# A decoder layer on one core: the scale columns' queue, 18 products of ones at the start, and four groups of small products moved by one or two steps

## The chip, the cores and the metric

The kernel runs on one core of a Trainium2 chip. Its time is the device time of one execution in microseconds (us); of several executions the median is given. Five engines work side by side, each with its own list of instructions: TensorE (PE, matmuls; PEld is its loading of weights), VectorE (DVE), ScalarE (ACT), GpSimd (POOL) and SyncE (SP, which here issues most of the transfers). An instruction starts when those ahead of it on its engine are through and the semaphores that it waits for have come.

## The reference, cut to what matters

One step of a hybrid decoder layer over 576 tokens: 512 of a new sequence and 8 x 8 of running ones, model width 2048.

```python
x += W_out @ [gated_delta_heads(8) | mlstm_heads(4)](rmsnorm(x) @ W_in)
x += conv_ffn(rmsnorm(x))         # W_up, causal conv, gate, W_down; d_ff = 5632
y  = rmsnorm(x)
# gated delta, chunks of 128 here: with k normalised and decays from the gates,
#   lower = strict(beta * k k^T * decay);  X = (I + lower)^-1
#   v_new = X (v - w S);  o = qe S + (q k^T * decay) v_new;  S = S * gl + kd^T v_new
# mlstm: the like, with a normaliser and a running maximum
# both again for the 64 sample tokens, each from its own stored state
```

The outputs are y and the new states of heads and convolutions. All is in 32-bit floats.

## The kernel before, in words

Every large product W x is taken apart into high and low halves of W and x (in a 32-bit format that TensorE reads at full rate), and three products hi·hi, hi·lo and lo·hi are added up. ScalarE casts a weight block `raw` to its high part `wh` (L120), VectorE subtracts to get the low part `wl` (L121); a block holds 8 k-tiles of 128 rows. The 576 tokens lie in two halves of 288 columns, so a **step**, one k-tile in `dense_part`, is six products (`three`, L200), and a dense tile of 128 output rows is 16 steps.

TensorE's order is the order in which the code issues (`manual_schedule`); the other engines' order is set by a scheduler from priorities and dependences. Between the dense products stand the small ones of the gates and heads, written as generators: after each step `tick()` lets each running generator go on until its next `yield n`, which makes it pause n ticks. So `yield n` sets by how many steps of dense work a small product stands behind what its operands come from. Small products write to four rotating PSUM tiles (`psr`).

`startup` (L360) loads the scale columns `g1` (2048 floats, 8 KB, on GpSimd's queue), sets `ones`, and then, for 16 activation tiles, loads x on SyncE's queue, scales it to `ah` on ScalarE (L384) and takes the rest `al` on VectorE (L385). The weight blocks are loaded after x tiles 1, 7 and 15. The gates' weights are scaled on GpSimd (L396).

`gate_rows` computes the gates of all heads: 64 products (L446) after 20 ticks, the squares' sum (L455), then a chain of small operations on rows, then two products with `there` (L520), whose operand comes from L511. Later it issues the gates' rows, on which the heads begin.

`dn_head` is one gated-delta head. It transposes k (L683; sample part L689 to L691), which ScalarE reads eight times (L686 and L687), builds `U` from k·k (L710), then KQ from k·q (L721), then transposes v (L732; sample part L737), pauses `YI` = 8 ticks while `inverse` works (L866 and L873 are its masks and sums), and then goes through the four chunks (L751, L758, L762 to L765). `dn_sample` (L832 to L846) does the sample tokens: L832, its ScalarE reader L833, the casts `vp` and `kp` (L797, in `pack`), masks `vm` on GpSimd (L806), and a product per pair of sequences (L846) that updates the state (L849). `ml_head` and `ml_sample` do the mLSTM heads; L1092 is the product for the samples' normaliser, L1040 a division of an output, L1044 a transposition of it.

Of the kernel before, what the change touches and what calls it, by code (L numbers as in the profile page):

```python
# [15 lines left out]
P = 128  # L16
D = 2048
KT = 16
# [20 lines left out]
OPA = 1600  # L39
YI = 8  # L40
YJ = 20


G1, G2, G3, CW, DG, MG, FW, FBI, GB, AL, M0, NPAR = 0, 16, 32, 48, 144, 145, 153, 417, 505, 506, 507, 515
# [22 lines left out]
class Layer:  # L67
# [292 lines left out]
    def startup(self):  # L360
        nc, I = self.nc, self.I
        self.par = self.cp.tile([P, NPAR], F32, tag="par", name="par")
        g1 = self.cp.tile([P, KT], F32, tag="g1", name="g1")
        nc.gpsimd.dma_start(out=g1, in_=I["par"][:, G1:G1 + KT])
        self.ones = self.cp.tile([P, P], F32, tag="ones", name="ones")
        nc.vector.memset(self.ones, 1.0)
        nc.scalar.activation(self.rstd_tile()[:, 0:1], self.ones[:, 0:1], AF.Copy)
        self.eps6 = self.cp.tile([P, 1], F32, tag="eps6", name="eps6")
        nc.vector.memset(self.eps6, EPS)
        self.epsh = self.cp.tile([P, 1], F32, tag="epsh", name="epsh")  # L370
        nc.vector.memset(self.epsh, EPS * EPS * P)

        self.xh, self.xl, self.xs = [], [], []
        self.gw = self.r(shape=[P, KT, 32])
        acts = [self.new_act(k) for k in reversed(range(KT))][::-1]
        for k in range(KT):
            x = self.r()
            self.xs.append(x)
            nc.sync.dma_start(out=x, in_=I["xT"][k])
            if k in (1, 7, 15):  # L380
                self.load_unit()
            hi, lo = acts[k]
            g = g1[:, k:k + 1]
            nc.scalar.activation(hi, x, AF.Copy, scale=g)  # L384
            nc.vector.scalar_tensor_tensor(out=lo, in0=x, scalar=g, in1=hi.bitcast(F32), op0=ALU.mult, op1=ALU.subtract)  # L385
            self.xh.append(hi)
            self.xl.append(lo)
        for k in range(0, KT, 4):
            self.gate_weights(k, g1)
        nc.sync.dma_start(out=self.par, in_=I["par"])  # L390
# [38 lines left out]
    def gate_rows(self):  # L429
        nc, I, O = self.nc, self.I, self.O  # L430
# [79 lines left out]
        for s, t in quarters:  # L510
            V.scalar_tensor_tensor(out=t5[s, t], in0=y[s], scalar=cq[s, 4:5], in1=val[s], op0=ALU.mult, op1=ALU.add)  # L511
        edge.__exit__(None, None, None)
        yield 12
        R1, R2, R3 = self.r(), self.r(), self.r()
        for t in (R1, R2, R3):
            Pl.memset(t, 0.0)
# [143 lines left out]
    def dn_head(self, h, q, k, v, sz):  # L660
        nc, I, O = self.nc, self.I, self.O
# [52 lines left out]
        res = []  # L714
        inv = self.inverse(U, res, 0)
        next(inv)
        yield 1
        pr = self.psr()
        for c in range(NCH):
            sl, n = self.blk(c)  # L720
# [12 lines left out]
        for c in range(NCH):  # L733
            sl, n = self.blk(c)
            A.activation(vs[:, sl], pv[:, sl], AF.Copy, scale=irk[:, c:c + 1])
        pv = self.psr()
        nc.tensor.transpose(pv[0:64, 0:P], v[:, sl4], self.ident)  # L737
        A.activation(vss, pv[0:64, 0:P], AF.Copy, scale=irk[0:64, 4:5])

        yield YI  # L740
        yield from inv
        X, Xs = res
        sample = self.spawn(self.dn_sample(h, st, k, qe, KQ, Xs, cjc(4), kds, vss, gl))
# [109 lines left out]
    def inverse(self, U, res, more):  # L853
# [44 lines left out]
        def masked(i):  # L898
            m = U if i == len(LV) - 1 else self.r()
            Pl.tensor_tensor(out=c4(m), in0=c4(U), in1=self.bc4(self.con[:, C_LV + P * i:C_LV + P * i + P]), op=ALU.mult)  # L900
            return m

        m = masked(0)
        yield YJ + more
        self.tc.cur_priority -= PR
# [166 lines left out]
    def ml_sample(self, h, caug, kws, sT, gl, finish):  # L1072
        nc, O = self.nc, self.O
        V, A, Pl, mm = nc.vector, nc.scalar, nc.gpsimd, nc.tensor.matmul
        sl = slice(SEQ, NT)
        yield 2
        qc = self.r(shape=[P, 2, 257])
        for g in range(2):
            pr = self.psr()
            for j in range(4):  # L1080
                mm(pr[32 * j:32 * j + 32, 0:257], self.qim[:, 4 * g + j], caug[g][:, j], start=True, stop=True)
            A.copy(qc[:, g], pr[:, 0:257])
        yield 2
        pn = self.psr()
        mm(pn[0:64, 0:257], sT[0:64, sl], self.vas, start=True, stop=False)
        for g in range(2):
            mm(pn[32 * g:32 * g + 32, 0:257], self.pick[:, 0], qc[:, g], start=False, stop=True)
        fin = self.spawn(finish(pn, 4))
        bmk = self.con[0:64, C_BM:C_BM + NB]
        yield 4  # L1090
        pm = self.psr()
        mm(pm[:, 0:NB], kws, bmk, start=True, stop=True)  # L1092
        for b in range(NB):
            n1 = caug[b // 4][:, b % 4, 256:257]
            V.scalar_tensor_tensor(out=n1, in0=n1, scalar=gl[:, 4 + b:5 + b], in1=pm[:, b:b + 1], op0=ALU.mult, op1=ALU.add)
        kp = self.pack(kws, P, "kp", ("hhl", "hhl"))
        vp = self.pack(self.vas, 256, "vp", ("hlh", "lhh"))
        for g in range(4):
            vm = self.masked_rows(vp, g // 2, g % 2 * 2, 2)
            yield W  # L1100
            pr = self.psr()
            mm(pr, kp[:, g // 2], vm, start=True, stop=True)
            for i in range(2):
                b = 2 * g + i
                cc = caug[b // 4][:, b % 4, 0:256]
                V.scalar_tensor_tensor(out=cc, in0=cc, scalar=gl[:, 4 + b:5 + b], in1=pr[:, 256 * i:256 * i + 256], op0=ALU.mult, op1=ALU.add)
        for g in range(2):
            self.later(6, O["sC"][h, g], caug[g])
        while not fin[3]:
            yield 1  # L1110
# [628 lines left out]
```

## Time and profile before

| | |
|---|---|
| median of 3 runs | 2661.66 us (2661.35 to 2661.88) |
| the profiled execution | 2660.97 us, span 2659.2 us |
| TensorE busy, whole span | 2628.2 us (99%) |
| TensorE busy, 139 to 860 us (heads) | 714.58 of 721 us |
| TensorE busy, 860 to 2110 us | 1249.01 of 1250 us |
| TensorE's first product | at 8.50 us |
| granted TensorE clock, mean | 0.998 |

The profile is one execution. The waits of an engine are listed as "line waited for, total, times, longest". A row of the timeline gives start, duration, engine, line, operation and tiles; in square brackets stands how long the engine was idle before, and what ended it. "xN" is a run of N equal instructions; a product of plain 32-bit floats shows as two rows of TensorE. The busy time of matmuls overlaps, so their pace is read from their starts.

### The profile page before, as it was taken

How to read it: one execution, taken by the hardware profiler on the slowest of the kernel's cores; microseconds unless marked ns; L12 is line 12 of the kernel's file. 1: busy time of each engine (PE TensorE's matmuls, PEld its weight loads, DVE VectorE, ACT ScalarE, POOL GpSimd, SP SyncE). 2: the span in 40 equal slices, each digit the busy share in tenths (PEclk: the TensorE clock that was granted, in tenths of full speed). 3: DMA queues.
4: the chain of work that ended last, by engine and by line, in shares of the span. 5: the costliest groups of instructions: out<-in, count | busy, mean ns of one | idle time of the engine just before them, and what ended most of it. 6: DMA issues, size and time to landing. Idle time of an engine off the chain costs nothing.

```text
span 2659.2 us, 49165 instructions
## 1 busy us (share of the span) xinstructions
PE 2628.2 (99%) x20061; PEld 2584.9 (97%) x20061; DVE 2057.7 (77%) x3448; ACT 1083.3 (41%) x1697; POOL 461.6 (17%) x670
## 2 busy tenths in 40 slices
PE   8999999999999999999999999999999999999998
PEld 8999999999999999999999999999999999999997
DVE  6676666667765455599999999999999998988656
ACT  5333433434434333244444444444444443434224
POOL 2222322322322001111212222222222200000001
PEclk9999999999999999999999999999999999999999
DMA  5242322422323434343333333333333463342332
GB/s 206 83 126 87 130 84 78 131 86 85 98 85 106 154 121 135 129 137 114 109 109 109 109 108 108 106 108 107 108 108 109 133 231 90 119 137 71 123 98 100
DMA packets 112682, 304.05 MB, mean 114 GB/s; under 512 B 21928, under 2 KB 28216, under 8 KB 112456
## 3 DMA queue, kind: packets, MB, share of 16 engines
q1 hardware_dynamic: 108616, 292.20, 34.2%
q0 software_dynamic: 1600, 6.35, 0.7%
q8 instruction: 157, 2.57, 0.4%
q10 hardware_dynamic: 2240, 2.36, 0.2%
q14 instruction: 69, 0.57, 0.1%
HBM read 262.44 MB, written 38.42 MB: 113 GB/s over the span
## 4 chain that ended last, share of the span: by engine, by line
PE 96%; DVE 2%; ACT 1%; issue 0%; POOL 0%; DMA 0%; DVEq 0%; POOLq 0%
PE pd L200 38%; PE pr L1358 33%; PE pd L1358 13%; PE pr L200 4%; PE pr L1588 1%; DVE r L1623 0%; PE pr L918 0%; PE pr L258 0%; DVE wl L121 0%; PE pr L721 0%; PE pr L758 0%; ACT r L686 0%; PE pr L930 0%; PE pr L1055 0%; ACT r L687 0%
## 5 line engine op out<-in xcount | busy, mean ns | idle before, releaser
L120 ACT CAST wh<-raw 128x1024 fp32r<-128x1024 f32 (+1 forms) x392 | 403.2, 1029 | 732.2 <-PE pd L200 391.6
L1358 PE MATMUL pr<-bh,wl 128*128 128x288 f32 x2248 | 663.3, 295 | 0.9 <-DVE wl L121 0.9
L1358 PE MATMUL pr<-bh,wh 128*128 128x288 f32 x2248 | 663.4, 295 | 0.3 <-ACT wh L120 0.3
L1358 PE MATMUL pr<-bl,wh 128*128 128x288 f32 x2248 | 663.3, 295 | 0.0
L121 DVE TENSOR_TENSOR wl<-raw,wh 128x1024 fp32r<-128x1024 f32 (+1 forms) x392 | 471.3, 1202 | 109.6 <-ACT wh L120 105.5
L200 PE MATMUL pd<-ah,wh 128*128 128x288 f32 x2304 | 512.9, 304 | 8.5 <-ACT wh L120 8.5
L200 PE MATMUL pd<-al,wh 128*128 128x288 f32 x2304 | 492.9, 295 | 0.0
L200 PE MATMUL pd<-ah,wl 128*128 128x288 f32 x2304 | 491.3, 294 | 0.0
L1358 PEld LDWEIGHTS pr<-bh,wl 128*128 128x128 f32 x2248 | 423.0, 188 | 1.9 <-DVE wl L121 1.9
L1358 PEld LDWEIGHTS pr<-bh,wh 128*128 128x128 f32 x2248 | 422.6, 188 | 0.5 <-ACT wh L120 0.5
L1358 PEld LDWEIGHTS pr<-bl,wh 128*128 128x128 f32 x2248 | 422.9, 188 | 0.1
L200 PEld LDWEIGHTS pd<-ah,wh 128*128 128x128 f32 x2304 | 367.1, 188 | 21.0 <-ACT wh L120 8.5
L200 PEld LDWEIGHTS pd<-ah,wl 128*128 128x128 f32 x2304 | 368.8, 188 | 0.3 <-DVE wl L121 0.3
L200 PEld LDWEIGHTS pd<-al,wh 128*128 128x128 f32 x2304 | 368.1, 188 | 0.0
L120 ACT CAST wh<-s 128x1024 fp32r<-128x1024 f32 (+1 forms) x180 | 178.8, 993 | 364.5 <-DVE s L1323 138.4
L1358 PE MATMUL pd<-bh,wl 128*128 128x288 f32 x888 | 262.1, 295 | 0.6 <-DVE wl L121 0.6
L1358 PE MATMUL pd<-bl,wh 128*128 128x288 f32 x888 | 262.2, 295 | 0.0
L1358 PE MATMUL pd<-bh,wh 128*128 128x288 f32 x888 | 262.0, 295 | 0.0
L1240 POOL COPY fst<-r 128x18 f32<-128x18 f32 x88 | 97.6, 1109 | 678.8 <-DVE r L1396 678.8
L121 DVE TENSOR_TENSOR wl<-s,wh 128x1024 fp32r<-128x1024 f32 (+1 forms) x180 | 206.5, 1147 | 6.8 <-ACT wh L120 2.2
L1358 PEld LDWEIGHTS pd<-bh,wl 128*128 128x128 f32 x888 | 167.1, 188 | 0.9 <-DVE wl L121 0.9
L1358 PEld LDWEIGHTS pd<-bl,wh 128*128 128x128 f32 x888 | 167.1, 188 | 0.0
(420 smaller groups left out, 3736.1 us busy)
## 6 DMA issues: line engine op xcount, KB each, us to landing
raw<-in_w_up SPq DMA_DIRECT2D x176, 512.0 KB
raw<-in_w_in SPq DMA_DIRECT2D x112, 512.0 KB
raw<-in_w_down SPq DMA_DIRECT2D x40, 512.0 KB
raw<-in_w_out SPq DMA_DIRECT2D x32, 512.0 KB
raw<-in_w_down SPq DMA_DIRECT2D x40, 384.0 KB
hid<-r SPq DMA_DIRECT2D x44, 288.0 KB
r<-hid SPq DMA_DIRECT2D x40, 288.0 KB
r<-in_xT SPq DMA_DIRECT2D x32, 288.0 KB
```

The costliest lines, as they stand in the source:

```text
L120: self.last_split = (nc.scalar.copy(hi, src), nc.vector.tensor_tensor(out=lo, in0=src, in1=hi.bitcast(F32), op=ALU.subtract))
L121: nc.vector.tensor_tensor(out=lo, in0=src, in1=hi.bitcast(F32), op=ALU.subtract))
L200: mm(outs[hf], w, x[:, hf * HALF:(hf + 1) * HALF], start=first and i == 0, stop=last and i == 2)
L1240: nc.gpsimd.tensor_copy(f, rb[:, 512:602].rearrange("p (b w) -> p b w", b=9)[:, :, 0:2])
L1358: mm(out, w[:, ks], x[:, sl], start=k == 0 and i == 0, stop=k == nk - 1 and i == 2)
L1588: mm(pr[:, 0:n], w[:, ks], acts[kk][:, a * NT + sl.start:a * NT + sl.stop], start=kk == 0 and i == 0, stop=kk == FB - 1 and i == 2)
```

## The change

Three edits. The load of `g1` is issued on ScalarE's queue. In `startup`, ahead of the first dense product, `NW` = 18 products of `ones` with `ones` (128x128) go to one PSUM tile that nobody reads. And pauses change: 12 to 14 ticks ahead of `there`; 1 to 2 ahead of KQ; two ticks ahead of the sample part of v's transposition, which the pause behind it gives back; 4 to 5 ahead of L1092. Lines from L364 on move by one, from L374 by five, and from L737 by six.

```diff
+NW = 18
...
-        nc.gpsimd.dma_start(out=g1, in_=I["par"][:, G1:G1 + KT])
+        nc.scalar.dma_start(out=g1, in_=I["par"][:, G1:G1 + KT])
...
+        pw = self.psr()
+        for _ in range(NW):
+            nc.tensor.matmul(pw[:, 0:P], self.ones, self.ones, start=True, stop=True)
...
         edge.__exit__(None, None, None)
-        yield 12
+        yield 14
         R1, R2, R3 = self.r(), self.r(), self.r()
...
         next(inv)
-        yield 1
+        yield 2
         pr = self.psr()
...
+        yield 2
         pv = self.psr()
         nc.tensor.transpose(pv[0:64, 0:P], v[:, sl4], self.ident)
         A.activation(vss, pv[0:64, 0:P], AF.Copy, scale=irk[0:64, 4:5])
...
-        yield YI
+        yield YI - 2
...
-        yield 4
+        yield 5
         pm = self.psr()
         mm(pm[:, 0:NB], kws, bmk, start=True, stop=True)
```

ScalarE at the start of the program, before and then now (`g` is the scale columns, `ah` a scaled activation tile, `wh` the first weight block's high part):

```order
L1722 UNCONDITIONAL_BRANCH
L367 ACT_TABLE_LOAD
L367 ACTIVATE rstd<-ones 128x1
L384 ACTIVATE ah_124<-r_126,g_83 128x576
L384 ACTIVATE ah_122<-r_130,g_83 128x576
L120 CAST wh_134<-raw_132 128x1024
```

```order
L1728 UNCONDITIONAL_BRANCH
L365 DMA g_83<-in_par 128x16
L368 ACT_TABLE_LOAD
L368 ACTIVATE rstd<-ones 128x1
L389 ACTIVATE ah_143<-r_145,g_83 128x576
L389 ACTIVATE ah_141<-r_149,g_83 128x576
L121 CAST wh_153<-raw_151 128x1024
```

The load of g now stands first on ScalarE, ahead of its table load; the rest follows in the order of before.

TensorE where the second head begins beside the first (the place of the wait at 214.82 us). Before, L832 belongs to the first head's sample job, L758 to L765 to its chunks, and L683 to L721 to the second head:

```order
L758 MATMUL pr_2519<-rr_2489,r_1874 128x128
...
L832 MATMUL pr_2528<-vss_1910,Xs_1876 64x128
L683 MATMUL pr_2553<-con,r_2100 128x128 x4
...
L710 MATMUL pr_2588<-r_2100 128x128 x4
L200 MATMUL pd_2404<-ah_102,wh_2332 128x288 x2
L200 MATMUL pd_2404<-al_103,wh_2332 128x288 x2
L200 MATMUL pd_2404<-ah_102,wl_2333 128x288 x2
L762 MATMUL pr_2619<-r_1909,r_1828 128x128
L764 MATMUL pr_2619<-r_1744,S_2455 128x128
L765 MATMUL pr_2619<-r_1746,r_1909 128x128
L721 MATMUL pr_2626<-r_1941,r_2100 128x128 x4
```

The same place now, with the lines' new numbers (L688 is L683, L715 L710, L838 L832, L768 L762, L726 L721):

```order
L764 MATMUL pr_2544<-rr_2514,r_1893 128x128
L688 MATMUL pr_2551<-con,r_2119 128x128 x4
...
L715 MATMUL pr_2586<-r_2119 128x128 x4
L838 MATMUL pr_2611<-vss_1935,Xs_1895 64x128
...
L201 MATMUL pd_2420<-ah_119,wh_2351 128x288 x2
L201 MATMUL pd_2420<-al_120,wh_2351 128x288 x2
L201 MATMUL pd_2420<-ah_119,wl_2352 128x288 x2
L768 MATMUL pr_2644<-r_1934,r_1847 128x128
L770 MATMUL pr_2644<-r_1758,S_2480 128x128
L771 MATMUL pr_2644<-r_1760,r_1934 128x128
L726 MATMUL pr_2651<-r_1960,r_2119 128x128 x4
```

The sample product L832 has moved from in front of the transpositions to a step behind them, and between the products with k (L710) and KQ (L721) stand two steps instead of one.

ScalarE at the same place, before and then now (L686 and L687, now L691 and L692, read the transposed k; L797, now L803, casts; L833, now L839, reads the sample product):

```order
L759 ACTIVATE r_1909<-pr_2519,cj_1851 128x128
L833 ACTIVATE vss_1910<-pr_2528,cj_1851 64x128
L797 CAST vp_2538<-vss_1910 32x128 x4
L686 ACTIVATE r_2551,ss_2549<-pr_2553 128x128
L692 ACTIVATE kds_2552,ss_2549<-pr_2566 64x128
...
L797 CAST kp_3336<-kds_2552 32x128
L687 ACTIVATE r_2551<-pr_2553,cols 128x128
L797 CAST kp_3336<-kds_2552 32x128 x2
```

```order
L765 ACTIVATE r_1934<-pr_2544,cj_1870 128x128
L691 ACTIVATE r_2549,ss_2547<-pr_2551 128x128
L692 ACTIVATE r_2549<-pr_2551,cols 128x128
...
L691 ACTIVATE r_2549,ss_2547<-pr_2551 128x128
L839 ACTIVATE vss_1935<-pr_2611,cj_1870 64x128
L692 ACTIVATE r_2549<-pr_2551,cols 128x128
L803 CAST vp_2621<-vss_1935 32x128 x4
L803 CAST kp_3361<-kds_2550 32x128 x4
```

The four casts of `vp` stood ahead of the readers of k and stand behind them now.

## The prediction, made before the changed kernel ran

> **What bounds the kernel now.** I read the profile's page first, then the waits of TensorE, then the timeline where the longest of these waits lie. From the page: span, busy time of each engine, and the chain that ended last.
>
> ```profile
> span 2659.2 us, 49165 instructions
> PE 2628.2 (99%) x20061; PEld 2584.9 (97%) x20061; DVE 2057.7 (77%) x3448; ACT 1083.3 (41%) x1697; POOL 461.6 (17%) x670
> PE 96%; DVE 2%; ACT 1%; issue 0%; POOL 0%; DMA 0%; DVEq 0%; POOLq 0%
> ```
>
> TensorE works 2628.2 of 2659.2 us, so this change can only win time in which TensorE is idle or runs at less than full speed. The waits of TensorE name that time (us in total, times, longest):
>
> ```profile
> PE pd L200 <- ACT wh L120: 8.5, 1, 8.5
> PE pr L721 <- ACT r L687: 3.8, 5, 0.8
> PE pr L737 <- POOL r L866: 0.9, 2, 0.5
> PE pr L1092 <- DVE hn L1040: 0.7, 2, 0.4
> PE pr L520 <- DVE r L511: 0.7, 1, 0.7
> PE pr L737 <- DVE r L703: 0.4, 1, 0.4
> PE pr L1044 <- DVE st L849: 0.3, 1, 0.3
> ```
>
> One wait of 8.5 us stands at the start, before any product. The other six rows, 6.8 us together, are small products of the gates and heads that stand ahead of their operand. The change touches all of these rows except L1044, which its other shifts move.
>
> The start, from the timeline (start, duration, engine, line):
>
> ```profile
> 0.74 1.28 ACT L367 ACT_TABLE_LOAD   x1 [0.74 <-PEq L1715]
> 0.84 0.17 DVE L366 MEMSET ones<- 128x128 f32 x1 [0.84 <-PEq L1715]
> 1.52 0.68 POOL L364 DMA_DIRECT2D g<-in_par  x1
> 5.03 0.72 SPq L129 DMA_DIRECT2D raw<-in_w_in  x1
> 5.92 6.68 SPq L379 DMA_DIRECT2D r<-in_xT  x8
> 13.08 0.33 SPq L129 DMA_DIRECT2D raw<-in_w_in  x1
> 6.07 1.44 ACT L384 ACTIVATE ah<-r,g 128x576 fp32r<-128x576 f32 x2 [3.83 <-DMA g<-in_par]
> 7.42 1.03 ACT L120 CAST wh<-raw 128x1024 fp32r<-128x1024 f32 x1
> 8.50 0.85 PE L200 MATMUL pd<-ah,wh 128*128 128x288 f32 x2 [8.50 <-ACT wh L120]
> 12.37 1.04 ACT L120 CAST wh<-raw 128x1024 fp32r<-128x1024 f32 x1
> 14.00 1.22 DVE L121 TENSOR_TENSOR wl<-raw,wh 128x1024 fp32r<-128x1024 f32 x1
> 15.13 5.92 DVE L385 SCALAR_TENSOR_TENSOR al<-r,g,ah 128x576 fp32r<-128x576 f32 x8
> 27.27 4.13 PE L446 MATMUL pr<-r,r 128*32 128x144 f32 x128
> 25.64 1.12 POOL L396 TENSOR_TENSOR r<-r,g 128x128 f32<-128x128 f32 x3
> ```
>
> The scale columns g land at 6.07, 4.55 us after their issue at 1.52; only then ScalarE scales two activation tiles and casts the first weights, and the first product runs at 8.50. The windows show what follows (window, its length, TensorE's busy time and rows):
>
> ```profile
> 8.50:12.33 3.83, 3.83 (x15) 1.00 1.03 404
> 12.33:23.20 10.87, 10.87 (x83) 1.00 1.04 399
> ```
>
> The first 15 recorded products take 0.255 us each, the next 83 take 0.131: half speed for the first 3.83 us, though the clock column reads 1.00 in both. That costs about 15 x 0.124 = 1.9 us.
>
> **The start, costed.** 18 products of ones go ahead of the first dense tile, and need only the memset that ends at 0.84 + 0.17 = 1.01. For a 128x128 product in this number format, and for the heads below, the rows of one head (216 us into the span):
>
> ```profile
> 209.69 0.36 ACT L833 ACTIVATE vss<-pr,cj 64x128 f32<-64x128 f32 x1 [0.79 <-PE pr L832]
> 210.08 1.26 ACT L797 CAST vp<-vss 32x128 fp32r<-32x128 f32 x4
> 214.40 0.37 ACT L687 ACTIVATE r<-pr,cols 128x128 f32<-128x128 f32 x1
> 214.82 1.16 PE L721 MATMUL pr<-r,r 128*128 128x128 f32 x8 [0.76 <-ACT r L687]
> 215.74 0.53 PE L200 MATMUL pd<-ah,wh 128*128 128x288 f32 x2
> 212.16 1.04 POOL L806 TENSOR_TENSOR vm<-vp,con 96x512 fp32r<-96x512 f32 x1 [0.28 <-ACT kds L692]
> 220.74 0.39 PE L846 MATMUL pr<-vm,kp 96*128 96x512 f32 x1
> ```
>
> Four products of L721 (eight rows) take 215.74 - 214.82 = 0.92 us, 0.23 each, so 0.46 at half speed. From about 1.1 us, 3.83 us of half speed hold 8.3 of them; the other 9.7 take 2.2; they end at about 7.15. The first weights: eight transfers are out at a time (I read this from SyncE's issues spreading out after the eighth), so the eleventh issue, at 5.92, says that the third, the first weights, has landed. Cast (1.03) they are ready at 7.0 if g lets ScalarE do its two tiles before. On ScalarE's queue g is issued at about 0.75, ahead of the table load, and at the same 4.55 us lands at 5.3: two tiles (1.44) and the cast follow until 7.8. So the first product runs at 7.2 to 7.8, at full speed, since the pause is under 0.7 us. The table load behind the issue has slack: ScalarE is idle until 6.07 today.
>
> What is late next is the second weight block, needed by the ninth step. It is the tenth transfer, which has landed when the eighteenth is issued: 5.92 + 6.68 - 0.33 (one issue) = 12.27. Cast (1.04) 13.3; its low part on VectorE (1.22) 14.55; the low part of the ninth activation tile (5.92 / 8 = 0.74) 15.3. TensorE gets there at 7.2 to 7.8 + 48 x 0.131 = 13.5 to 14.1 and waits about 1.1. From 15.3 there are 46 rows left, 6.1 us: the first dense tile ends at 21.4 instead of 23.2. The gates' products (L446) follow five steps later, at 25.5 instead of 27.27; their second group of weights on GpSimd, the first of the three at 25.64 + 0.37, is asked for a us after that, so it holds nothing up. **Start: -1.8.** Bounds: if g lands at 6.07 as today, VectorE keeps its order and the ninth low tile is ready at 15.13 + 0.74 = 15.87: -1.2. If the products of ones don't open the clock, they end at 1.1 + 18 x 0.46 = 9.4 and it is +0.9. The other way, without the ninth tile's wait, -2.4.
>
> [...] The trace has 404 GB/s moved just after g has landed, and nothing that shows g's own part of its 4.55 us. [...] The sum stays at -1.8, as the ninth tile decides.
>
> **The heads, costed.** A step is six products, 6 x 0.131 = 0.79 us.
> - L520 stands two steps later, 1.6 us against a wait of 0.7: **-0.7**.
> - L721 waited five times, 3.8. Ahead of its last reader (214.40 + 0.37) ScalarE cast vp for the other head's sample job (1.26). The gates' two extra steps turn the two heads against each other: in the new order the eight readers of pk stand ahead of those casts, and TensorE has one more step between. Lateness 0.76 becomes 0.76 - 1.26 - 0.79 = 1.3 us to spare. **-3.8**.
> - L737 stands two steps behind L732, 1.6 us against waits of at most 0.5: **-1.3**.
> - L1092 stands one step later, 0.79 against 0.4. L1044 stands ahead of it now, and what it waited for, a state update that ended on its heels, moves away by the gates' two steps as L721's readers do: **-1.1**, at worst 0.
> - New waits: the order of VectorE and ScalarE moves in all twelve heads (eight and four). I followed the new order by hand with the rows' durations and found places with 0.2 to 0.9 us to spare, and one where the first mLSTM head's updates now stand behind a dense tile's evacuation and a weights' low part. I put **+1.1** for these, bounds 0 and 2.5 (three of the longest waits of today).
>
> Sum: -1.8 - 0.7 - 3.8 - 1.3 - 1.1 + 1.1 = **-7.6 us**. The profiled execution took 2660.97 (span 2659.2 and 1.8 around it), 0.7 under the median of 2661.66; the median becomes **2654.1**. A measurement of this kernel tells 0.2%, 5.3 us, from no change: the line is 2656.3.
>
> **Rivals.**
> - *The waits come back at the next group.* For it: VectorE is 77% busy, and L762, L768 and the casts lie within a us of their readers. If each of L721's five, L737's three and L1092's two returned at two thirds, 6.2 x 2/3 = 4.1 comes back instead of 1.1: 2657.1. Against: the readers gain the whole 1.26 of the casts. Chance 0.14, no change.
> - *The change doesn't do what it says:* the readers are still behind the casts, and L721's 3.8 stays: 2657.9. The order speaks against it. Chance 0.04, no change.
> - *The start gives nothing:* clock not open, or g as late: 2661.7 - 5.8 to -7.0 = 2654.7 to 2655.9. [...] Chance 0.12, mostly still faster.
> - *Slower:* the sample chain. Its casts now come behind the eight readers, some 4.3 us later, and masks (1.04 on GpSimd, done at 213.20) and the product L846 (220.74) hang on them. Today 7.5 us lie between, and L846 stands a step later, so some 4 are left. It decides once the chain is over 4 us longer than I count; at 2 us for each of eight heads it gives 2654.1 + 16 = 2670. Chance 0.04.
> - My forecast, both parts with new waits of 0 to 2.5: 2653.0 to 2655.5. Chance 0.66.
>
> Range: from the forecast's low end with the start's other bound, 2653.0 - 0.6 = 2652.4, to past the returning waits and the readers still behind, 2658.0. Faster 0.75 (0.66 and most of the start's 0.12), same 0.20, slower 0.05 with 0.01 for what I haven't named.
>
> **What would show it.** Right: L200's wait for ACT wh is gone from the first product, which runs at 7.2 to 7.8 and at 0.13 from the first; a wait of about 1 us for VectorE's ninth low tile; L446 at about 25.5; no rows for L721, L737, L520 among TensorE's waits (by their new lines). Wrong: a run of waits of the same size at the products L762, L846 or L1054 of each head, or half-speed products after 7.8 us. Waits of over 4 us in sum in the heads would make it no change.

## The result, and the profile after

The changed kernel takes 2669.45 us (median of 8 runs, 2665.92 to 2671.9); the kernel before took 2661.61 beside it (8 runs, 2660.79 to 2662.44). The ratio is 1.003, 95% interval 1.0019 to 1.004: 7.8 us slower, where the prediction had 7.6 us faster. The new kernel also scatters more from run to run, over 6.0 us against 1.7.

First the page of the changed kernel: span, busy times, and the chain that ended last.

```profile
span 2667.1 us, 49246 instructions
PE 2634.7 (99%) x20097; PEld 2591.5 (97%) x20097; DVE 2070.4 (78%) x3448; ACT 1083.1 (41%) x1697; POOL 457.7 (17%) x669
PE 90%; DVE 5%; issue 2%; DMA 1%; ACT 1%; POOL 1%; SPq 0%; DVEq 0%; POOLq 0%; ACTq 0%
```

The span is 7.9 us longer. VectorE is busy for 12.7 us more with the same number of instructions, so some of them take longer; and 5% of the chain that ended last now runs over VectorE, against 2%. TensorE's waits say where (line, releaser, total, times, longest; the lines are the new ones):

```profile
PE pr L743 <- DVE r L727: 6.8, 5, 1.9
PE pr L764 <- DVE rr L759: 4.6, 5, 1.9
PE pd L201 <- DVE wl L122: 2.5, 2, 2.0
PE pr L768 <- DVE hn L1046: 1.2, 2, 0.6
PE pd L201 <- DVE al L390: 0.8, 1, 0.8
```

All the waits that were to go are gone: no row for L726 (L721 before), L525 (L520), L1098 (L1092) or L1050 (L1044), and L743 no longer waits for L866 or L703. In their place stand 12.6 us for VectorE in the heads (L743, L764, L768) and 2.0 after them. L743 is the one that the change moved.

The start did as planned in this execution. In the timeline of the changed kernel: the products of ones, g's landing, the first product, the wait for the ninth low tile, the gates' first product.

```profile
1.06 5.84 PE L377 MATMUL pr<-ones 128*128 128x128 f32 x36 [1.06 <-DVE epsh L372]
3.97 1.44 ACT L389 ACTIVATE ah<-r,g 128x576 fp32r<-128x576 f32 x2 [1.30 <-DMA g<-in_par]
6.93 0.53 PE L201 MATMUL pd<-ah,wh 128*128 128x288 f32 x2
15.43 0.54 PE L201 MATMUL pd<-al,wh 128*128 128x288 f32 x2 [0.78 <-DVE al L390]
25.68 4.13 PE L451 MATMUL pr<-r,r 128*32 128x144 f32 x128
```

The gates' products begin at 25.68 instead of 27.27: 1.6 us won in these two executions. The place moves from one execution to the next: over the ten traces here that have both edits of the start it lies between 24.93 and 27.67 (half of them within 25.3 to 25.7), and without g on ScalarE's queue at 27.12 to 28.25 in three.

The heads, at the place of the old wait at 214.82 us. VectorE in the changed kernel:

```profile
214.06 1.08 DVE L805 TENSOR_TENSOR vp<-vss,vp 32x128 fp32r<-32x128 f32 x1
215.18 0.35 DVE L774 SCALAR_TENSOR_TENSOR S<-S,last,pr 128x128 f32<-128x128 f32 x1
215.44 2.39 DVE L879 TENSOR_TENSOR r<-r 128x256 f32<-128x256 f32 x1
217.76 0.68 DVE L727 TENSOR_TENSOR r<-pr,r 128x512 f32<-128x512 f32 x1
```

GpSimd and TensorE beside it:

```profile
212.78 1.22 POOL L871 TENSOR_TENSOR r<-r,con 128x512 f32<-128x512 f32 x1 [0.68 <-DVE r L879]
213.97 1.03 POOL L812 TENSOR_TENSOR vm<-vp,con 96x512 fp32r<-96x512 f32 x1
215.29 1.04 POOL L812 TENSOR_TENSOR vm<-vp,con 96x512 fp32r<-96x512 f32 x1 [0.29 <-DVE vp L805]
216.29 1.26 POOL L906 TENSOR_TENSOR r<-r,con 128x512 f32<-128x512 f32 x1
211.65 1.06 PE L726 MATMUL pr<-r,r 128*128 128x128 f32 x8
218.49 0.30 PE L743 MATMUL pr<-con,r 128*64 128x128 f32 x1 [1.74 <-DVE r L727]
```

Before, the same stretch of GpSimd and VectorE read:

```profile
210.84 1.04 POOL L806 TENSOR_TENSOR vm<-vp,con 96x512 fp32r<-96x512 f32 x1 [3.72 <-ACT vp L797]
211.05 0.97 DVE L799 TENSOR_TENSOR vp<-vss,vp 32x128 fp32r<-32x128 f32 x1 [0.36 <-ACT vp L797]
217.65 1.23 POOL L865 TENSOR_TENSOR r<-r,con 128x512 f32<-128x512 f32 x1 [0.68 <-DVE r L873]
218.84 0.67 DVE L722 TENSOR_TENSOR r<-pr,r 128x512 f32<-128x512 f32 x1
218.84 1.28 POOL L900 TENSOR_TENSOR r<-r,con 128x512 f32<-128x512 f32 x1
219.44 1.29 DVE L873 TENSOR_TENSOR r<-r 128x256 f32<-128x256 f32 x2
```

The older head's sample job has come a step later, and its casts stand behind the readers of k. So its subtractions L805 and GpSimd's masks L812 now fall between the younger head's operations: GpSimd is busy without a pause longer than 0.3 us from 212.78 to 217.55, and VectorE's L879 on 128x256 takes 2.39 us, where it takes 0.42 in `no_mask` below, and ends 0.28 behind L906. Behind it L727, which reads KQ out of PSUM, runs 6.1 us after its products began (217.76 - 211.65), where it was 4.0 before (218.84 - 214.82, both from the rows shown). L743 waits for that read. It asks for the rotating PSUM tile that KQ was written to, four tiles on.

The waits at L764 have the same look. The longest of them:

```profile
431.40 1.76 DVE L122 TENSOR_TENSOR wl<-raw,wh 128x1024 fp32r<-128x1024 f32 x1
433.08 1.26 DVE L896 TENSOR_TENSOR r<-r 40x44 f32<-40x44 f32 x1
432.29 1.99 POOL L906 TENSOR_TENSOR r<-r,con 128x512 f32<-128x512 f32 x1
434.65 0.49 PE L764 MATMUL pr<-rr,r 128*128 128x128 f32 x2 [1.93 <-DVE rr L759]
```

L122 takes 1.22 us elsewhere and L896 of this shape 0.18 (at 428.02). Beside L906, a mask of the inverse on GpSimd, they take 1.76 and 1.26. Both stand ahead of L759, for which L764 waits, so 1.6 us of its 1.93 are this stretching.

Another loss stands behind the heads. In the changed kernel, VectorE at the head of the next phase:

```profile
869.75 3.35 DVE L1172 RECIPROCAL ratio<-rstd 128x512 f32<-128x512 f32 x1 [5.79 <-DMA out_sC<-st]
874.35 1.22 DVE L122 TENSOR_TENSOR wl<-raw,wh 128x1024 fp32r<-128x1024 f32 x1
```

By the profile the reciprocal waits for a store of the mLSTM state; its output `ratio` takes over memory of the heads. VectorE stands for 5.79 us, the weights' low part behind it comes late, and TensorE waits 2.01 at 875.63. Before, the last head's norm stood ahead of the reciprocal, which ran at 860.41 without a wait.

The sum: removed are 1.6 at the start and the waits of 0.7, 3.8, 1.3 and 1.1, together 8.5. New are 6.8 + 4.6 + 1.2 + 2.0 + 0.3 (one at L924) = 14.9, and 1.5 of half speed (last section). That leaves +7.9.

### The profile page after: what moved, and what is told of

It reads as the page before. It is cut to its first block, busy times and chain, and to the rows that moved or that the text cites. A ratio compares the mean times of both kernels' runs of the same rounds, so it can differ in the third digit from the quotient of the medians.

```text
span 2667.1 us, 49246 instructions
## 1 busy us (share of the span) xinstructions
PE 2634.7 (99%) x20097; PEld 2591.5 (97%) x20097; DVE 2070.4 (78%) x3448; ACT 1083.1 (41%) x1697; POOL 457.7 (17%) x669
## 4 chain that ended last, share of the span: by engine, by line
PE 90%; DVE 5%; issue 2%; DMA 1%; ACT 1%; POOL 1%; SPq 0%; DVEq 0%; POOLq 0%; ACTq 0%
PE pd L201 34%; PE pr L1364 33%; PE pd L1364 13%; PE pr L201 3%; PE pr L1594 1%; DVE wl L122 1%; DVE bl L122 0%; DVE vp L805 0%; ACT wh L121 0%; DVE r L1629 0%; DVE r L879 0%; PE pr L924 0%; DMA raw<-in_w_in 0%; PE pr L936 0%; DVE r L896 0%
## 5 line engine op out<-in xcount | busy, mean ns | idle before, releaser
L122 DVE TENSOR_TENSOR wl<-raw,wh 128x1024 fp32r<-128x1024 f32 (+1 forms) x392 | 473.7, 1208 | 96.9 <-ACT wh L121 92.3
L201 PEld LDWEIGHTS pd<-ah,wh 128*128 128x128 f32 x2304 | 368.2, 189 | 15.1 <-issue 8.3
L122 DVE TENSOR_TENSOR wl<-s,wh 128x1024 fp32r<-128x1024 f32 (+1 forms) x180 | 206.5, 1147 | 6.6 <-ACT wh L121 1.8
```

Of the source, the lines that this page charges most:

```text
L122: nc.vector.tensor_tensor(out=lo, in0=src, in1=hi.bitcast(F32), op=ALU.subtract))
L201: mm(outs[hf], w, x[:, hf * HALF:(hf + 1) * HALF], start=first and i == 0, stop=last and i == 2)
```

## The experiments

Each is timed beside the kernel before on the same chip. `start` to `gate_back` had a "before" of 2661.88, `kq_back` to `no_mask` 2661.95, the rest 2661.58. I began with two theories of the loss, A (a PSUM tile used again too soon) and B (the gates' extra ticks); both fell in the first four runs, and C took their place. Differences between two of these runs are told by their medians; an interval of the ratio is 0.0009 to 0.0013 to either side, 2.4 to 3.5 us, so a difference of 1 or 2 us is not resolved by the times alone.

**start**: the change without its four pauses.

```diff
-        yield 14          # and 2 ahead of KQ, 2 ahead of v's sample part, 5 ahead of L1092
+        yield 12          # and 1, 0, 4 as before
```

> The start's two edits alone (g on ScalarE's queue, 18 products of ones), all pauses as before. Theory A (the loss is a bank: the sample transposition of v now takes the PSUM tile of KQ, which VectorE has not read yet) and theory B (the gates' two extra ticks turn the heads against each other, so that VectorE's small operations fall beside GpSimd's and VectorE is late everywhere) both leave the start its gain of 1.6 us, the shift of the first gate product in the trace: 2660.0, between 2659.5 and 2660.5. If the start itself disturbs the heads (a third theory, by its earlier clock of VectorE and GpSimd), it is above 2662.

2659.87 us (11 runs), ratio 0.9992 (0.9983 to 1.0001). The median is as expected to 0.1 us: all of the loss is in the pauses.

**pauses**: the four pauses without the start.

```diff
-        nc.scalar.dma_start(out=g1, in_=I["par"][:, G1:G1 + KT])
+        nc.gpsimd.dma_start(out=g1, in_=I["par"][:, G1:G1 + KT])
-        for _ in range(NW):
-            nc.tensor.matmul(pw[:, 0:P], self.ones, self.ones, start=True, stop=True)
```

> All pauses of the change, without the start's two edits. A and B: the change's 2669.5 and 1.6 more, 2671.0, with the waits at L743 and L764 in the heads. If start and pauses only hurt together, below 2664.

2675.81 us, ratio 1.0053 (1.004 to 1.0066). The direction holds, the size is 4.8 us more than expected. Its trace has the same waits (6.8 at L743's product, 5.8 at L764's) and two more stretches of half speed.

**v_back**: the change without v's shift.

```diff
-        yield 2
         pv = self.psr()
...
-        yield YI - 2
+        yield YI
```

> The change without the shift of the sample transposition of v (its two ticks back behind it). A: L743's 6.8 us go, the 1.3 us of the old place come back, and L764's 4.6, which come after it in VectorE's queue, go in part: 2661 to 2664. B: VectorE is as late as before, so the next products wait in its place: 2667 or more.

2672.44 us, ratio 1.0039 (1.0025 to 1.0052). A falls: without the shift it is no faster. Its two longest waits in sum:

```profile
PE pr L844 <- ACT r L776: 9.7, 5, 2.1
PE pr L763 <- DVE rr L758: 2.7, 2, 1.8
```

The next product that needs a PSUM tile waits instead, for a read of ScalarE that in turn stands behind VectorE's update of S. The tile only names who notices. TensorE is also busy for 5.8 us more than in the changed kernel (2640.5 against 2634.7): half speed behind five of its waits (last section).

**gate_back**: the change with the gates' pause as before.

```diff
-        yield 14
+        yield 12
         R1, R2, R3 = self.r(), self.r(), self.r()
```

> The change with 12 ticks ahead of the gates' products, as in the kernel before; all else stays. B: the heads stand to each other as in the kernel before, VectorE's busy time falls from 2070 back to about 2058 us, L743 and L764 wait for under 2 us together: 2653 to 2659. A: the bank is the same, so L743 still waits: 2667 or more.

2672.24 us, ratio 1.0038 (1.0026 to 1.0051). B falls too: L743 waits 6.7, L764 5.1. All heads begin on the gates' rows, but what shifts one head against the next is a pause inside a head.

**kq_back**: the change with KQ's pause as before.

```diff
         next(inv)
-        yield 2
+        yield 1
```

> The change with one tick ahead of KQ's products, as in the kernel before; start, gates' pause, v's shift and the mLSTM pause stay. Theory C (the extra tick ahead of KQ moves the older head's sample job by a step, so its casts, subtractions and GpSimd's masks fall into the younger head's chain on VectorE): VectorE's busy time falls back to about 2058 us, L743's and L764's waits go, L721's 3.7 us return: start 2659.9, less 0.7, 1.2 and 0.7, 2657 to 2658. Theory A (v's shift puts two uses of a bank too close): L743 still waits, 2663 or more.

2659.5 us (11 runs), ratio 0.9993 (0.9984 to 1.0002). Waits of this kernel:

```profile
PE pr L726 <- ACT r L692: 3.7, 5, 0.8
PE pr L924 <- issue: 2.4, 3, 1.0
PE pr L1050 <- DVE hn L1046: 0.8, 2, 0.4
```

The loss is gone and L721's wait is back, as theory C says. VectorE's busy time is 2059.9 us. The time is 2 us over the expected 2657 to 2658: L924, the inverse's first product, waits 2.4 (the profile's "issue" says that it shows no releaser; `start_v` below comes back to it), and the mLSTM pause wins nothing, since L1050 waits 0.8 where L1092 waited 0.7.

**kq_only**: the start and KQ's pause alone.

```diff
-        yield 14          # and 2 ahead of v's sample part, 5 ahead of L1092
+        yield 12          # and 0, 4 as before; 2 ahead of KQ stays
```

> The start's two edits and the extra tick ahead of KQ, the other pauses as before. C: the whole loss is here: 2659.9 less L721's 3.7, and some 14 to 17 of new waits: 2670 to 2674. A: 2656, since L743 is where it was.

2672.76 us, ratio 1.0041 (1.0028 to 1.0053), as C expects. This one tick costs 12.9 us against `start`. In the traces it is not waits alone: L844 waits 9.5 us in five waits and L1049 2.6 in two, and TensorE is busy for 5.9 us more than in `start` with the same products (2638.7 against 2632.8), as three of L844's waits are followed by half speed. With the other three pauses beside it (the change itself) the loss is 3.3 us smaller, at the edge of the noise, and only one wait is followed by half speed.

**v_bank**: the change with v's sample tile taken earlier.

```diff
-        yield 2
         pv = self.psr()
+        yield 2
         nc.tensor.transpose(pv[0:64, 0:P], v[:, sl4], self.ident)
```

> The change, but the PSUM tile for the sample transposition of v is taken ahead of its two ticks, so that it is no longer the one that KQ was written to. The order on all engines stays but for the tiles' turn. A: L743's 6.8 us go: 2662 to 2664. C: VectorE is as late as before, and the wait moves to the next product that needs it: 2667 or more.

2670.96 us, ratio 1.0034 (1.0022 to 1.0046). L743 still waits 6.9, for the same reader L727. But this run does not test A, since the tiles' turn did not change. Had v's sample part taken its tile ahead of the two ticks, L845 would have had the one of L768 to L771, and these are the rows:

```profile
214.38 0.43 PE L845 MATMUL pr<-r,vss 64*128 64x64 f32 x2
216.06 0.27 ACT L777 COPY r<-pr 128x128 f32<-128x128 f32 x1 [2.07 <-DVE S L774]
```

L845 runs 1.95 us before L777 has read that tile (214.38 against 216.33). In `v_back`, where v's sample part does take its tile ahead of that product, the product (L844 there) waits for that read (L776 there). So `v_bank` is in effect the changed kernel once more. A falls by `v_back`, where the wait only moves, and by `kq_back` and `start_v`, where v's shift stands and no product waits for KQ's reader.

**no_mask**: the change without the masks of the gated-delta sample job.

```diff
-        vms = [self.masked_rows(vp, g, 0, 4) for g in range(2)]
+        vms = [vp[:, g].unsqueeze(1).to_broadcast([96, 4, P]) for g in range(2)]
```

> The change without the masks of the gated-delta sample job: its state products read the unmasked rows, so the states of the samples are not the reference's. VectorE's order is the same; only GpSimd's two operations of 1.04 us per head are gone. C, if GpSimd is what stretches VectorE: L879 on 128x256 falls from 1.34 us to under 0.8, L805 on vp from 0.82 to 0.4, L743's wait is under 2 us in all, and the time is 2660 to 2664. If the queue's order alone is at fault, the durations hardly move and it stays above 2667.

2661.57 us (11 runs), ratio 0.9998 (0.9989 to 1.0007). VectorE and GpSimd at the place shown above, some 2 us later in this run:

```profile
216.04 1.32 DVE L805 TENSOR_TENSOR vp<-vss,vp 32x128 fp32r<-32x128 f32 x1
217.39 0.35 DVE L774 SCALAR_TENSOR_TENSOR S<-S,last,pr 128x128 f32<-128x128 f32 x1
217.65 0.42 DVE L879 TENSOR_TENSOR r<-r 128x256 f32<-128x256 f32 x1
215.94 1.27 POOL L906 TENSOR_TENSOR r<-r,con 128x512 f32<-128x512 f32 x1
218.73 0.30 PE L743 MATMUL pr<-con,r 128*64 128x128 f32 x1
```

VectorE does the same operations in the same order, but GpSimd is through with L906 at 217.21 and L879 takes 0.42 instead of 2.39. The mean of the eight heads' L879 on 128x256 falls from 1.34 to 0.41, and L743 doesn't wait at all. L805 did not fall as far as expected (0.82 to 0.68): one of the two now runs beside L906. So without two GpSimd operations per head the changed kernel is 7.9 us faster, some 1.5 of it because no wait of TensorE is followed by half speed here, as one was there. What is left is L764 (5.3 us in three waits), whose operand stands in VectorE's queue behind the inverse's small operations and a weights' low part, and these too are stretched beside GpSimd: at 429.78 L122 takes 2.35 instead of 1.22, beside the inverse's mask L906 (429.76, 1.29), which this run keeps. Another 5.0 us go to weights, 1.2 of them ahead of the first product and 2.3 behind the reciprocal, which waits 6.05 for a store.

The group of these L879 on the page of VectorE's forms, in the kernel before, in the changed one and without masks, one row each:

```profile
L873 DVE TENSOR_TENSOR r<-r 128x256 f32<-128x256 f32 x8 | 4.4, 547 | 0.0
```

```profile
L879 DVE TENSOR_TENSOR r<-r 128x256 f32<-128x256 f32 x8 | 10.7, 1342 | 0.0
```

```profile
L879 DVE TENSOR_TENSOR r<-r 128x256 f32<-128x256 f32 x8 | 3.3, 413 | 0.0
```

**start_v**: the start and v's shift.

```diff
-        yield 14          # and 2 ahead of KQ, 5 ahead of L1092
+        yield 12          # and 1, 4 as before; 2 ahead of v's sample part stays
```

> The start's two edits and the shift of the sample transposition of v, all other pauses as before. Theory D (the shift gains nothing, since the inverse's first product, L918 in the kernel before, stands 0.1 us behind VectorE's transposition that it reads, and any us that TensorE wins ahead of it is waited for there): L742's 1.2 us go, and L923's wait grows from 0.2 to over 1: 2659 to 2660, as the start alone. Rival: the shift is worth its 1.2 us, 2658.6, and L924's 2.4 us in the run with KQ's pause put back came from another pause.

2659.62 us (11 runs), ratio 0.9992 (0.9983 to 1.0001): the time can't tell 1.2 us from nothing, but the trace bears theory D out. The wait that `start` has at L742 (1.2) is gone, and L924 waits for 0.64, 0.61 and 0.72. In the kernel before, VectorE's transposition for that product ended at 176.94 and the product ran at 177.04, 0.1 us behind it; here the transposition ends at 177.34, and the product runs at 177.45 after its wait of 0.64. What TensorE wins ahead of it is waited for there.

**start_gate**: the start and the gates' pause.

```diff
-        yield 2           # ahead of KQ; 2 ahead of v's sample part, 5 ahead of L1092
+        yield 1           # and 0, 4 as before; 14 ahead of the gates stays
```

> The start's two edits and 14 ticks ahead of the gates' products. The wait of 0.7 us goes and nothing else moves: 2659.1, 0.7 under the start alone. By D's reasoning it could be waited for again where the heads begin; then 2659.9.

2658.99 us (11 runs), ratio 0.9989 (0.998 to 0.9998). Its median is the lowest of all, 2.6 us under the kernel before, and it is the only run below 1 whose interval leaves out 1. Whether the gates' pause pays is not shown: 0.9 us under `start` is within the noise, and in the trace the gates' wait of 0.7 is gone, but L742 waits 1.8 instead of 1.2.

**g_only** and **ones_only**: one half of the start each, all pauses as before.

```diff
+        nc.scalar.dma_start(out=g1, in_=I["par"][:, G1:G1 + KT])    # g_only: this, no products of ones
+            nc.tensor.matmul(pw[:, 0:P], self.ones, self.ones, start=True, stop=True)   # ones_only: this, g on GpSimd's queue
```

> Only g on ScalarE's queue. The prediction's sum: the first product runs at 7.0 and at half speed for 3.8 us, the ninth step is reached at about 15.2, when its low tile is ready, and the gates' products start at 25.4 to 25.7, as with both edits: 2659.9. If the half speed costs its 1.9 us as before: 26.0, and 2660.4.

> Only the 18 products of ones. The first product waits for g as in the kernel before, until 8.5, and then runs at full speed; the ninth step waits for its low tile until 15.9: gates' products at 26.1, 1.2 us won, 2660.5. If the clock closes again between the last product of ones at 6.9 and 8.5, the first tile runs at half speed again and nothing is won: 27.3.

2659.91 us, ratio 0.9994 (0.9985 to 1.0003), and 2660.82 us, ratio 0.9995 (0.9986 to 1.0004). First product and gates' products of `g_only`, then of `ones_only`:

```profile
7.17 0.85 PE L201 MATMUL pd<-ah,wh 128*128 128x288 f32 x2 [7.17 <-ACT wh L121]
25.84 4.13 PE L448 MATMUL pr<-r,r 128*32 128x144 f32 x128
```

```profile
9.37 0.53 PE L201 MATMUL pd<-ah,wh 128*128 128x288 f32 x2 [1.56 <-ACT wh L121]
27.12 4.13 PE L451 MATMUL pr<-r,r 128*32 128x144 f32 x128
```

The times don't separate the two halves. The traces speak for g: `g_only` reaches the gates' products as early as the runs with both edits, and its half speed is spent while the ninth tile isn't there anyway (its ninth step begins at 15.44; the ninth low tile is the first of four that VectorE makes from 14.37 on in 3.00 us, so ready at about 15.1). `ones_only` missed its 26.1: g landed at 6.94, 0.87 later than in the kernel before, and the first product had to wait for it. The first product takes 0.53 for two rows, as at full speed (0.85 in the kernel before), so half speed did not come back over the 1.56 us between. That is the half of the expectation that held, and it won next to nothing: the gates' products begin at 27.12, where the kernel before had 27.27.

## Why the prediction was wrong, point by point

- **The start**: the ninth tile decides, as predicted, and the size agrees in this execution (-1.6 against -1.8); `start`'s median is 2.0 under the kernel before, with an interval that just takes in 1. First product at 6.93 (7.2 to 7.8), wait for the ninth low tile 0.78 (about 1.1), L451 at 25.68 (25.5). The reading that eight transfers are out at a time fits: in all eleven traces with g on ScalarE's queue the first weights' cast starts within 0.01 us of SyncE's eleventh issue (5.83 and 5.83 in the changed kernel, 7.27 and 7.26 in `kq_only`), and the changed kernel casts the second block at 12.34, 0.01 behind the eighteenth issue (12.33). g landed at 3.97, earlier than I had put it, so that no longer g but the first weights or the last product of ones decide when the first product runs: between 6.85 and 8.36 in these traces. The products of ones took 0.44 each at half speed, from 1.06 to 4.39 (15 rows), and then 0.22 each until 6.90; a dense product, with 288 columns in the halves' format, took 0.13. That half speed lasts a time, and not a number of products, was my estimate from the 3.83 us (15 rows) of the trace before; it lasted 3.33 us here and in `g_only` 3.35 (7.17 to 10.52, 12 rows). But the sum gave no credit to the two halves apart, and no run shows a gain of the ones once g is early.
- **The waits to be removed**: right, all of them went from the places where they were.
- **"The gates' two extra steps turn the two heads against each other"**: this step failed. `gate_back` has the same new waits without these steps, and with them but without KQ's tick L721's wait stays (3.7 in `kq_back`, 3.8 in `start_gate`). The tick ahead of KQ turned the heads.
- **New waits, "bounds 0 and 2.5"**: this is the term that made the sum wrong. It stands at +1.1, and the new waits were 14.9: 13.8 us more. The 1.5 us of half speed behind one of them had no term at all. I had asked only whether the casts get out of the readers' way, not on whom they fall: they and GpSimd's masks landed in the younger head's chain on VectorE. I followed VectorE's new order with the durations of the old trace, and these did not hold beside a busy GpSimd: L879 took 1.34 us in the mean instead of 0.55. The trace of before had the hint: L799 takes 0.28 us at 210.41 and 0.97 at 211.05, beside L806 (rows above). The 7.5 us of slack that I counted for the sample chain were about who waits for the masks, not about what the masks hold up.
- **The rival "the waits come back at the next group"** came nearest: waits did return at other products because VectorE was late. It did not see why VectorE would be late, and held the price to two thirds of what was removed. The slower rival named the sample chain, but put its price at L846, which did not wait; its price was VectorE. I gave slower 0.05.
- **v's shift and the mLSTM pause** show no gain even without the tick (`start_v`, `kq_back`): one is waited for again at L924, which had 0.1 us to spare, the other at L1050.
- The reciprocal's wait for a store was not in the prediction at all. Scatter is explained in part: half speed follows some waits and not others (next section).

The cause is settled as far as these runs go: KQ's tick costs 12.9 us, and without two GpSimd operations per head the changed kernel is 7.9 us faster. How the rest divides between VectorE's order, the inverse's own masks on GpSimd and the reciprocal was not tested by itself; in `kq_only` the reciprocal waits 4.54 us for a store and no long wait of TensorE follows. Whether a fifth rotating PSUM tile would take up VectorE's lateness was not run either.

## What to carry to other kernels

A pause that takes a small product out of a wait moves everything behind it in its job. Here the price was on VectorE, which does the job's other work (busy for 2070.4 us instead of 2057.7): ask what that work now runs beside, on VectorE and GpSimd together, before counting the wait as won. Durations from a trace need not hold beside other neighbours: L879 on 128x256 took 0.55 us in the mean before, 1.34 after the change and 0.41 without the masks. Of several edits of one kind, time each alone: here one of four cost all, and of the other three none shows a gain clear of the noise, as what they won was mostly waited for again a little later.

## What the runs showed of the hardware that I had not expected

**VectorE's L879 took longer beside GpSimd, its reader of KQ did not.** L879 (two operands in SBUF) took 2.39 us beside GpSimd's L812 and L906 and 0.42 in `no_mask`, where L906 was through before it began. The reader of KQ has one operand in PSUM: in the kernel before, L722 took 0.67 at 218.84 while GpSimd's L900 ran from 218.84 for 1.28, and in the changed kernel (L727) it took 0.68 with GpSimd idle. What holds the one up and not the other, no run shows.

**Half speed followed some waits of about 2 us and not others.** The changed kernel after its wait of 1.86 us, and the window of the slow stretch (length, TensorE's busy time and rows, and so on; the third number from the end is the granted clock):

```profile
764.08 0.30 PE L743 MATMUL pr<-con,r 128*64 128x128 f32 x1 [1.86 <-DVE r L727]
765.25 0.46 PE L201 MATMUL pd<-ah,wh 128*128 128x288 f32 x2
768.18 0.83 PE L201 MATMUL pd<-ah,wh 128*128 128x288 f32 x2
769.14 0.43 PE L201 MATMUL pd<-ah,wl 128*128 128x288 f32 x2
765.50:768.80 3.30, 3.30 (x16) 3.30 (x15) 3.10 (x9) 0.23 (x1) 0.00 (x0) 0.50 0.31 66
```

From 765.5 to 768.8 a product takes 0.24 instead of 0.13, at a granted clock of 0.50, which costs 1.5 us. Of the five waits of 1.74 to 2.01 us in this execution only this one was followed by half speed; of the seven of 1.79 to 2.45 in `v_back` five were; of the five of 1.82 to 1.97 in `kq_only` three; in `no_mask` none of three of 2.12 to 2.44. The wait's length alone does not decide it: the one of 1.86 was followed by half speed, the one of 2.44 was not. What does, no run shows.

**g came 2.1 us earlier for 0.8 us of earlier issue.** g was there 3.2 us after its issue on ScalarE's queue (0.74 to 3.97), and 4.55 and 5.4 us after it on GpSimd's. It is no luck of one execution: in the eleven traces with g on ScalarE's queue its reader starts at 3.83 to 3.98, in the three on GpSimd's at 6.07, 6.83 and 6.94. The issue itself moved by 0.8 (1.52 to 0.74). Whether the queue gives the rest, or that g is now issued ahead of most of the x tiles, no run separates.
